# Rounding the weights' first part by a GpSimd casting transfer instead of ScalarE's copy

## The chip, the cores and the metric

The kernel runs on one core of one Trainium2 chip. The metric is the device time of one execution in microseconds (us), as the median of several runs. A profile is one separate execution with the hardware profiler on.

## The reference

Two layers of a hybrid model act on 256 context tokens and 256 latent tokens, each 2048 wide. A layer normalises and modulates its input to `u`, multiplies it by one wide weight matrix, sends groups of the product's columns through three mixers (a gated linear recurrence, a windowed attention, a state-space scan), and multiplies their joined outputs by a second matrix:

```python
u_l = rmsnorm(x, norm_w) * (1.0 + scale_l[:, None]) + shift_l[:, None]
u_c = rmsnorm(ctx_h, norm_w) * (1.0 + scale_c) + shift_c
lx_c, lg_c, q_c, k_c, v_c, ag_c, xbc_c, z_c, dt_c = split_cols(u_c @ w_in)
lx_l, lg_l, q_l, k_l, v_l, ag_l, xbc_l, z_l, dt_l = split_cols(u_l @ w_in)
lru_c, lru_l = rglru_mixer(...)
att_c, att_l = window_attention(...)
ssd_c, ssd_l = ssd_mixer(...)
mix_l = concatenate([lru_l * silu(lg_l), att_l * silu(ag_l), ssd_l])
x_new = x + gate_l[:, None] * (mix_l @ w_out)
if update_ctx:                       # every layer but the last
    mix_c = concatenate([lru_c * silu(lg_c), att_c * silu(ag_c), ssd_c])
    ctx_h = ctx_h + gate_c * (mix_c @ w_out)
```

The modulation (`scale`, `shift`, `gate`) is itself a product of a condition vector with a third, 2048 by 6144 matrix per layer.

## The kernel before

**Three products for one.** All data are 32-bit floats. For the two large products every operand is split into a first part, rounded to the format `float32r`, and a second part, the rest (also `float32r`). `mm3` then makes three matmuls per 128x128 weight block: first part by `u`'s first part, first part by `u`'s second part, second part by `u`'s first part.

**The weight stream.** `blocks` brings the weights in program order, in halves of a 128x1024 tile: 128 partitions by 512 columns, that is four weight blocks, 256 KB. There are 640 halves: 224 for `w_in` and 96 for `w_out` in each of two layers. For each half SyncE (SP) issues a load into a buffer `raw` (5 of them), ScalarE (ACT) copies `raw` to `hi` with rounding (line 242; 4 buffers), and VectorE (DVE) writes `lo = raw - hi` (line 243; 4 buffers). TensorE (PE) runs 12 matmuls on a half. `hi` and `lo` are free again when the last of them is done, `raw` when the subtraction is done. In the first layer a matmul has 512 columns; in the second most have 256, since the context half is not needed for `C`, `lg`, `z`, `q`, `ag` and for all of `w_out`. Here such halves are called narrow, the others wide.

**Stages.** In each layer the columns `B`, `C`, `x` come first, then `lx` and `lg` in turns (the recurrence, while the state-space core runs beside it), `z`, `k`, `v`, then `q` and `ag` in turns (attention), then `w_out` in three parts. In the first layer the modulation's weights are read while the first columns run (`ada_rows`, tiles `ar`), and `ada_wide` reads 256 more blocks of 256 KB (tiles `araw`) through VectorE later on.

**What sets the order.** PE's order is the program's: a planner with its own clock and a table of due times (`WAIT`) decides after each weight block which mixer step comes next. The other engines' orders are made by the scheduler when the program is built, from its own timeline; each engine then runs its list strictly in order. GpSimd (POOL) has 174 elementwise steps before the change, among them the recurrence's product (line 732), two steps on its result (744, 754), sums of squares (432), the attention's scaling of `prob` (873). All transfers are issued by SP.

The change touches `SHARED` (buffer counts), `blocks` and one call in `layer`. Lines behind `blocks` stand three higher in the changed kernel: 243 becomes 246, 732 becomes 735.

Of the kernel before, what the change touches and what calls it, by code (L numbers as in the profile page):

```python
# [9 lines left out]
F32R = mybir.dt.float32r  # L10
AF = mybir.ActivationFunctionType
# [3 lines left out]
P = 128  # L15
# [75 lines left out]
NW = KT * 7 * 8 // 8  # L91
# [20 lines left out]

SHARED = {}
for _tag, _bufs, _roles in [
        ("raw", 5, ("raw",)),
        ("ta", 4, ("lt0", "lt1", "prob", "xsw", "ar1")),
        ("tb", 2, ("cv", "qw", "v", "sq")),
        ("tc", 3, ("lh0", "lh1", "xs", "stage", "ar2")),
        ("td", 4, ("ao", "xc", "la2", "lgt", "agt", "cth", "diag", "dts", "xw", "dtraw", "rt1", "awsb", "cond32")),
        ("te", 1, ("rb", "ptch", "ssq")),  # L120
        ("t4", 3, ("BT", "CT", "Btok", "vh", "vl", "ptlh", "ar0")),
        ("bc", 4, ("bc", "dtw", "kh0", "kh1", "adac")),
        ("aw", 3, ("araw", "ww", "part0")),
        ("ee", 2, ("ee", "kl0", "kl1", "ar4")),
        ("H", 3, ("H", "ptll", "ptcl", "ar3")),
        ("bd", 2, ("gw", "qh", "ql", "part1")),
        ("sm", 6, ("spe", "sps", "spq", "dtr", "dtz", "dta", "acsT", "asb", "condt", "cond", "ea", "nlam", "cbm"))]:
    for _r in _roles:
        SHARED[_r] = (_tag, _bufs)


HB = 4
MIXERS_FIRST = {"lru_x": 150, "ssd_core": 150}
WAIT = {"B": (36.48, 14.89), "C": (28.19, 0.27), "x": (33.09, 10.71), "dt": (16.92, 0.59), "softplus":
        (19.41, 30.37), "acs": (0.94, 0.68), "core": (4, 5.2), "ada": (2.38, 5.97), "ada1": (1.17, 2.75), "z":
# [5 lines left out]
class Kernel:  # L141
# [88 lines left out]
        return self.cst[:, o:o + w]  # L230


    def blocks(self, src, n_tiles):
        nc = self.nc
        for i in range(n_tiles):
            whole = src[i].rearrange("p (b c) -> p b c", b=8)
            for h in range(2):
                part = self.t([P, 4, P], "raw")
                nc.sync.dma_start(out=part, in_=whole[:, 4 * h:4 * h + 4])
                hi = self.t([P, 4, P], "hi", HB, F32R)  # L240
                lo = self.t([P, 4, P], "lo", HB, F32R)
                nc.scalar.activation(out=hi, in_=part, func=AF.Copy)  # L242
                nc.vector.tensor_tensor(out=lo, in0=part, in1=hi.bitcast(F32), op=ALU.subtract)  # L243
                for b in range(4):
                    yield hi[:, b], lo[:, b]
# [709 lines left out]
    def layer(self, l, xs):  # L955
# [4 lines left out]
        self.core_done = False  # L960
        self.lru_h, self.att_o, self.parts_done, self.mixes = {}, {}, set(), {}
        t0 = lambda kind: 0 if l == 0 or kind in CTX_COLS else C
        wst = self.blocks(self.a["w_in"][l], NW)
        us = []

        rows = None
# [315 lines left out]
```

## Time and profile before

| what | value |
|---|---|
| median of 3 runs | 1828.84 us (1825.97 to 1830.53) |
| the profiled execution | 1825.69 us |
| its span in the trace | 1823.7 us |
| PE busy | 1762.9 us, 97% |
| DVE busy | 1406.0 us, 77% |
| ACT busy | 972.9 us, 53% |
| POOL busy | 215.5 us, 12% |
| transfers | 322.99 MB, mean 177 GB/s |

How to read it: busy times are of one profiled execution, and instructions that only issue transfers are not counted as busy. A busy PE is not a PE at its peak. A wait of an engine costs time only if PE, which carries the weight stream from the first half to the last, gets later by it.

### The profile page before, as it was taken

How to read it: one execution, taken by the hardware profiler on the slowest of the kernel's cores; microseconds unless marked ns; L12 is line 12 of the kernel's file. 1: busy time of each engine (PE TensorE's matmuls, PEld its weight loads, DVE VectorE, ACT ScalarE, POOL GpSimd, SP SyncE). 2: the span in 40 equal slices, each digit the busy share in tenths (PEclk: the TensorE clock that was granted, in tenths of full speed). 3: DMA queues.
4: the chain of work that ended last, by engine and by line, in shares of the span. 5: the costliest groups of instructions: out<-in, count | busy, mean ns of one | idle time of the engine just before them, and what ended most of it. 6: DMA issues, size and time to landing. Idle time of an engine off the chain costs nothing.

```text
span 1823.7 us, 30174 instructions
## 1 busy us (share of the span) xinstructions
PE 1762.9 (97%) x10522; PEld 1449.8 (79%) x10522; DVE 1406.0 (77%) x3117; ACT 972.9 (53%) x1798; POOL 215.5 (12%) x179
## 2 busy tenths in 40 slices
PE   7999999999999999999999999999989999999999
PEld 4677876667778778887888887888767788999999
DVE  4447769898898888889999536877788785788665
ACT  4324578688523354555232335544788863678443
POOL 0000111111110021212000020001122120121000
PEclk9999999999999999999999999999999999999999
DMA  9982333334675645557777433464343564554655
GB/s 359 389 299 66 123 104 104 122 122 144 230 222 179 189 153 184 173 174 239 229 225 225 144 122 107 140 197 148 99 134 113 173 220 137 182 180 153 218 185 179
DMA packets 186343, 322.99 MB, mean 177 GB/s; under 512 B 19120, under 2 KB 44624, under 8 KB 185552
## 3 DMA queue, kind: packets, MB, share of 16 engines
q1 hardware_dynamic: 186192, 321.09, 54.0%
q8 instruction: 82, 1.34, 0.3%
q14 instruction: 69, 0.57, 0.1%
HBM read 310.38 MB, written 10.63 MB: 176 GB/s over the span
## 4 chain that ended last, share of the span: by engine, by line
PE 71%; DVE 9%; issue 8%; ACT 6%; DMA 5%; POOL 1%; SPq 0%; ACTq 0%; DVEq 0%; POOLq 0%
PE acc L175 56%; PE mx L175 12%; PE ada L175 2%; DVE lo L243 2%; DMA bc<-acsD 2%; PE mx L171 1%; DVE araw L385 1%; ACT hi L242 1%; DVE ada L385 1%; DVE lh L735 1%; DMA araw<-in_adaw_dram 1%; DMA ar<-in_ada_dram 1%; DVE ee L1170 1%; ACT ww L1172 1%; ACT lt L717 1%
## 5 line engine op out<-in xcount | busy, mean ns | idle before, releaser
L175 PE MATMUL acc<-u,hi 128*128 128x512 f32 (+1 forms) x4800 | 1278.0, 355 | 3.8 <-ACT u L457 3.0
L175 PEld LDWEIGHTS acc<-u,hi 128*128 128x128 f32 x4800 | 837.5, 190 | 149.4 <-issue 33.2
L175 PE MATMUL acc<-u,lo 128*128 128x512 f32 (+1 forms) x2400 | 843.0, 351 | 7.9 <-DVE lo L243 7.8
L242 ACT ACTIVATE hi<-raw 128x512 fp32r<-128x512 f32 x640 | 397.5, 628 | 536.4 <-PE acc L175 401.3
L243 DVE TENSOR_TENSOR lo<-raw,hi 128x512 fp32r<-128x512 f32 x640 | 456.8, 717 | 185.9 <-ACT hi L242 175.3
L175 PEld LDWEIGHTS acc<-u,lo 128*128 128x128 f32 x2400 | 455.4, 190 | 73.1 <-DVE lo L243 12.9
L385 DVE SCALAR_TENSOR_TENSOR araw<-araw,adac 128x512 f32<-128x512 f32 x256 | 184.3, 720 | 6.2 <-DMA araw<-in_adaw_dram 3.9
L385 DVE SCALAR_TENSOR_TENSOR ada<-araw,adac 128x512 f32<-128x512 f32 x192 | 140.1, 730 | 13.2 <-DMA araw<-in_adaw_dram 6.7
L175 PE MATMUL mx<-u,hi 128*128 128x512 f32 (+1 forms) x320 | 98.8, 392 | 0.0
L1082 DVE SCALAR_TENSOR_TENSOR X<-acc,mod,X 128x256 f32<-128x256 f32 x144 | 65.0, 478 | 40.2 <-PE acc L175 40.2
L732 POOL TENSOR_TENSOR lt<-lt,ltl 128x512 f32<-128x512 f32 x32 | 45.9, 1457 | 327.2 <-ACT ltl L729 304.9
L873 POOL TENSOR_SCALAR prob<-prob,qrs 128x512 f32<-128x512 f32 (+1 forms) x48 | 58.2, 1228 | 214.0 <-ACT hi L242 123.9
L432 POOL TENSOR_TENSOR ssq<-ssq,sq 128x512 f32<-128x512 f32 (+1 forms) x26 | 34.0, 1310 | 308.1 <-ACT sq L428 308.1
L175 PEld LDWEIGHTS mx<-u,hi 128*128 128x128 f32 x320 | 55.9, 188 | 14.0 <-issue 4.6
L175 PE MATMUL mx<-u,lo 128*128 128x512 f32 (+1 forms) x160 | 60.7, 379 | 0.0
L516 POOL TENSOR_SCALAR X<-xs,prm 128x512 f32<-128x512 f32 (+1 forms) x16 | 16.3, 1024 | 362.0 <-DVE xs L494 357.5
L175 PE MATMUL mx<-xc,gw 64*64 64x512 f32 x128 | 41.7, 622 | 8.8 <-ACT lt L717 5.3
L428 ACT ACTIVATE sq<-X 128x256 f32<-128x256 f32 (+1 forms) x44 | 18.8, 452 | 54.5 <-DVE X L659 52.8
L1170 DVE SCALAR_TENSOR_TENSOR ee<-bc,nacs,ee 128x128 f32<-128x128 f32 x96 | 34.8, 418 | 14.8 <-DMA bc<-acsD 9.1
L776 POOL TENSOR_TENSOR qw<-qw,cst 128x256 f32<-128x256 f32 x20 | 23.1, 1156 | 195.6 <-DVE rt L775 168.9
L717 ACT ACTIVATE lt<-mx,gbh 128x512 f32<-128x512 f32 x64 | 42.2, 674 | 4.1 <-PE mx L175 4.0
L1169 ACT ACTIVATE ee<-bc,nacs 128x128 f32<-128x128 f32 x96 | 30.6, 391 | 17.7 <-DMA bc<-acsD 17.7
(240 smaller groups left out, 1946.1 us busy)
## 6 DMA issues: line engine op xcount, KB each, us to landing
raw<-in_w_in_dram SPq DMA_DIRECT2D x448, 256.0 KB, 2.8
araw<-in_adaw_dram SPq DMA_DIRECT2D x256, 256.0 KB, 3.1
raw<-in_w_out_dram SPq DMA_DIRECT2D x192, 256.0 KB, 3.0
ar<-in_ada_dram SPq DMA_DIRECT2D x84, 256.0 KB, 5.4
bc<-acsD SPq DMA_DIRECT2D x48, 256.0 KB, 3.9
ar<-in_ada_dram SPq DMA_DIRECT2D x22, 512.0 KB, 7.0
adac<-condD SPq DMA_DIRECT2D x28, 256.0 KB, 4.4
gw<-in_gates_dram SPq DMA_DIRECT2D x16, 256.0 KB, 2.9
```

The lines of the kernel that those rows point to most:

```text
L175: self.nc.tensor.matmul(out=out, lhsT=lhsT, rhs=rhs, start=start, stop=stop, **kw)
L242: nc.scalar.activation(out=hi, in_=part, func=AF.Copy)
L243: nc.vector.tensor_tensor(out=lo, in0=part, in1=hi.bitcast(F32), op=ALU.subtract)
L385: i = nc.vector.scalar_tensor_tensor(out=o, in0=raw, scalar=1.0, in1=row[c].rearrange("p t x -> p (t x)"), op0=ALU.mult, op1=ALU.mult, acc ...
L432: nc.gpsimd.tensor_tensor(out=self.ssq[0], in0=self.ssq[0], in1=sq, op=ALU.add)
L717: nc.scalar.activation(out=t, in_=pg[g], func=AF.Tanh, scale=0.5, bias=self.gb[:, 16 * g + 8 * d + m:16 * g + 8 * d + m + 1])
L732: nc.gpsimd.tensor_tensor(out=ti, in0=ti, in1=tl[:, d], op=ALU.mult)
L776: nc.gpsimd.tensor_tensor(out=dst, in0=src, in1=self.con("cos"), op=ALU.mult)
L873: nc.gpsimd.tensor_scalar(out=pr[j], in0=pr[j], scalar1=rs[:, j:j + 1], scalar2=1.0, op0=ALU.mult, op1=ALU.mult)
L1082: nc.vector.scalar_tensor_tensor(out=x[:, s], in0=acc[:, s.start - w0:s.stop - w0], scalar=mod[:, 2 * KT + m, c:c + 1], in1=x[:, s], op0=A ...
L1169: nc.scalar.activation(out=e[:, j], in_=bcs[0][:, j], func=AF.Identity, bias=k.nacs[:, f:f + 1])
L1170: nc.vector.scalar_tensor_tensor(out=e[:, j], in0=bcs[1][:, j], scalar=k.nacs[:, r:r + 1], in1=e[:, j], op0=ALU.add, op1=ALU.min)
```

## The change

`blocks` gets a number `own`. In tiles below it ACT rounds as before. In all others GpSimd issues a second transfer of the same half from DRAM into `hi`, whose destination type is `float32r`; the transfer itself casts. The subtraction on VectorE stays and now waits for two transfers. `own` is 20 tiles (40 halves) for the first layer's `w_in` and 0 for the second layer's `w_in` and for both `w_out`, so 600 of 640 halves take the new way. `raw` goes from 5 buffers to 3, `hi` from 4 to 6, `lo` stays at 4.

```diff
-        ("raw", 5, ("raw",)),
+        ("raw", 3, ("raw",)),
-HB = 4
-    def blocks(self, src, n_tiles):
+    def blocks(self, src, n_tiles, own=0):
                 part = self.t([P, 4, P], "raw")
                 nc.sync.dma_start(out=part, in_=whole[:, 4 * h:4 * h + 4])
-                hi = self.t([P, 4, P], "hi", HB, F32R)
-                lo = self.t([P, 4, P], "lo", HB, F32R)
-                nc.scalar.activation(out=hi, in_=part, func=AF.Copy)
+                hi = self.t([P, 4, P], "hi", 6, F32R)
+                lo = self.t([P, 4, P], "lo", 4, F32R)
+                if i < own:
+                    nc.scalar.activation(out=hi, in_=part, func=AF.Copy)
+                else:
+                    nc.gpsimd.dma_start(out=hi, in_=whole[:, 4 * h:4 * h + 4])
                 nc.vector.tensor_tensor(out=lo, in0=part, in1=hi.bitcast(F32), op=ALU.subtract)
-        wst = self.blocks(self.a["w_in"][l], NW)
+        wst = self.blocks(self.a["w_in"][l], NW, 0 if l else 20)
```

PE's list keeps its order. ACT's list in the second layer's recurrence: `lt`, `ltl` and `la` are the recurrence's gates, `bc` and `ee` belong to the state-space core, `hi` is the weights' first part. Before:

```order
L722 ACTIVATE ltl_13251<-lt_2949_13258,s_2638_11797 128x512
L717 ACTIVATE lt_2957_13286<-mx_13280,gbh_11799 128x512
L717 ACTIVATE lt_2958_13288<-mx_13281,gbh_11799 128x512
L723 ACTIVATE lt_2949_13258<-lt_2949_13258,s_2638_11797 128x512
L722 ACTIVATE ltl_13251<-lt_2957_13286,s_2638_11797 128x512
L242 ACTIVATE hi_13428<-raw_13426 128x512
L725 ACTIVATE la_2951_13264<-lt_2949_13258 128x512
L242 ACTIVATE hi_13450<-raw_13448 128x512
L723 ACTIVATE lt_2957_13286<-lt_2957_13286,s_2638_11797 128x512
L242 ACTIVATE hi_13468<-raw_13466 128x512
L725 ACTIVATE la_2959_13292<-lt_2957_13286 128x512
```

The same engine and place in the changed kernel:

```order
L725 ACTIVATE ltl_13251<-lt_2949_13258,s_2638_11797 128x512
L1178 ACTIVATE ee_13315<-ee_13315 128x512
L1183 ACTIVATE bc_13313<-bc_13313 128x512
L720 ACTIVATE lt_2957_13286<-mx_13280,gbh_11799 128x512
L726 ACTIVATE lt_2949_13258<-lt_2949_13258,s_2638_11797 128x512
L720 ACTIVATE lt_2958_13288<-mx_13281,gbh_11799 128x512
L725 ACTIVATE ltl_13251<-lt_2957_13286,s_2638_11797 128x512
L728 ACTIVATE la_2951_13264<-lt_2949_13258 128x512
L726 ACTIVATE lt_2957_13286<-lt_2957_13286,s_2638_11797 128x512
L728 ACTIVATE la_2959_13292<-lt_2957_13286 128x512
```

The copies to `hi` are gone from between the gates' steps.

POOL's list at the end of the second layer's recurrence, in the stage of `z`: `lt`, `lh` are the recurrence's tiles, `ssq` a sum of squares. Before:

```order
L732 TENSOR_TENSOR lt_3175_14363<-lt_3175_14363,ltl_14354 128x512
L732 TENSOR_TENSOR lt_3180_14385<-lt_3180_14385,ltl_14354 128x512
L744 TENSOR_TENSOR lh_3182_14395<-lh_3182_14395,lh_3183_14398 128x256
L754 TENSOR_TENSOR lh_3182_14395<-lh_3182_14395,lgt_14254 128x256
L432 TENSOR_TENSOR ssq_14575<-ssq_14575,sq_14675 128x256
```

The same engine and place in the changed kernel:

```order
L245 DMA hi_14554<-in_w_in_dram 128x512
L245 DMA hi_14580<-in_w_in_dram 128x512
L735 TENSOR_TENSOR lt_3175_14363<-lt_3175_14363,ltl_14354 128x512
L735 TENSOR_TENSOR lt_3180_14385<-lt_3180_14385,ltl_14354 128x512
L245 DMA hi_14598<-in_w_in_dram 128x512
L245 DMA hi_14616<-in_w_in_dram 128x512
L245 DMA hi_14634<-in_w_in_dram 128x512
L245 DMA hi_14681<-in_w_in_dram 128x512
L747 TENSOR_TENSOR lh_3182_14395<-lh_3182_14395,lh_3183_14398 128x256
L245 DMA hi_14726<-in_w_in_dram 128x512
L245 DMA hi_14744<-in_w_in_dram 128x512
L757 TENSOR_TENSOR lh_3182_14395<-lh_3182_14395,lgt_14254 128x256
```

The weight transfers now stand between the elementwise steps, before and behind each of them; `hi_14598` is the 398th of the 600, half number 437 counted from 0. The second such place, the product of `lt_3236` and `lt_3248`, has the 411th behind it, half number 450.

## Rows read from the trace of the kernel before

**Rows 1.** The page's head and its first part: busy us, share, instructions of an engine.

```profile
span 1823.7 us, 30174 instructions
PE 1762.9 (97%) x10522; PEld 1449.8 (79%) x10522; DVE 1406.0 (77%) x3117; ACT 972.9 (53%) x1798; POOL 215.5 (12%) x179
```

**Rows 2.** Stretches: length, each engine's busy us (instructions), PE's granted clock, DMA share, GB/s.

```profile
45.00:91.00 46.00, 45.07 (x500) 32.14 (x499) 22.16 (x59) 14.37 (x30) 0.00 (x0) 1.00 1.04 389
182.00:500.00 318.00, 306.85 (x1562) 227.85 (x1561) 265.98 (x529) 227.40 (x428) 52.36 (x40) 0.98 0.42 135
500.00:900.00 400.00, 389.02 (x1897) 321.87 (x1896) 356.70 (x903) 176.63 (x331) 59.46 (x48) 1.00 0.60 192
1100.00:1300.00 200.00, 195.03 (x972) 161.68 (x971) 146.54 (x322) 101.92 (x190) 12.53 (x11) 0.98 0.45 144
1300.00:1500.00 200.00, 184.65 (x1228) 146.61 (x1227) 169.53 (x298) 158.79 (x283) 43.16 (x37) 0.99 0.46 151
1700.00:1823.00 123.00, 120.36 (x1004) 120.15 (x1002) 78.54 (x131) 52.85 (x88) 0.00 (x0) 1.00 0.59 185
```

**Rows 3.** The page's groups: busy us, mean ns of one, idle before and releaser.

```profile
L242 ACT ACTIVATE hi<-raw 128x512 fp32r<-128x512 f32 x640 | 397.5, 628 | 536.4 <-PE acc L175 401.3
L243 DVE TENSOR_TENSOR lo<-raw,hi 128x512 fp32r<-128x512 f32 x640 | 456.8, 717 | 185.9 <-ACT hi L242 175.3
L732 POOL TENSOR_TENSOR lt<-lt,ltl 128x512 f32<-128x512 f32 x32 | 45.9, 1457 | 327.2 <-ACT ltl L729 304.9
```

**Rows 4.** Line 242 alone, in two stretches: ACT's busy us, clock, DMA share, GB/s.

```profile
182.00:500.00 318.00, 51.48 (x84) 0.98 0.42 135
1300.00:1500.00 200.00, 44.70 (x76) 0.99 0.46 151
```

**Rows 5.** The chain of waits from 1300 to 1500 us, shares by line.

```profile
by line: PE acc L175 23.7%; issue 20.1%; DVE lo L243 6.6%; DVE lh L735 5.0%; ACT hi L242 4.8%; PE mx L175 3.6%; DMA bc<-acsD 3.4%; DMA X<-xD 3.1%; ACT L729 2.5%; ACT lt L717 2.1%; DVE xc L471 2.1%; ACT ltl L729 1.9%; DVE lh L738 1.8%; ACT l
```

**Rows 6.** Transfers: the queue (packets, MB, share) and the weights' issues (median us to landing).

```profile
q1 hardware_dynamic: 186192, 321.09, 54.0%
...
raw<-in_w_in_dram SPq DMA_DIRECT2D x448, 256.0 KB, 2.8
...
raw<-in_w_out_dram SPq DMA_DIRECT2D x192, 256.0 KB, 3.0
```

**Rows 7.** POOL in order of time, stage of `z` in layer two: start, length, [idle before].

```profile
1454.54 2.99 POOL L732 TENSOR_TENSOR lt<-lt,ltl 128x512 f32<-128x512 f32 x2 [14.21 <-ACT ltl L729]
...
1478.71 3.01 POOL L732 TENSOR_TENSOR lt<-lt,ltl 128x512 f32<-128x512 f32 x2 [3.87 <-ACT ltl L729]
```

**Rows 8.** Instructions that touch `hi`, counted from the start: PE first (8 a half).

```profile
0.00:1459.40 1459.40, 1063.36 (x3496) 636.83 (x3497) 311.03 (x437) 271.65 (x439) 0.99 0.54 176
0.00:1481.90 1481.90, 1082.47 (x3600) 653.02 (x3601) 321.02 (x450) 279.47 (x452) 0.99 0.54 176
```

**Rows 9.** Instructions that touch `acc` in both `w_out` stages: PE, then weight loads.

```profile
900.00:950.00 50.00, 50.00 (x222) 41.42 (x221) 7.15 (x17) 0.00 (x0) 1.00 0.75 237
...
1700.00:1720.00 20.00, 20.00 (x170) 20.00 (x168) 3.31 (x7) 0.00 (x0) 1.00 0.57 180
```

**Rows 10.** Tile `raw` from 1700 us on: lengths in ns min/median/max, landing in us.

```profile
L243 DVE TENSOR_TENSOR lo<-raw,hi x81: 678/693/693, 1700.0 to 1815.2; 128x512 fp32r<-128x512 f32 x81
...
L239 SPq DMA_DIRECT2D raw<-in_w_out_dram x76: 327/328/489, 1700.7 to 1808.7; - x76
...
DMA to landing us min/median/max: 2.5/3.0/4.4
```

**Rows 11.** What PE waited for: us in total, times, longest us.

```profile
PE mx L175 <- ACT lt L717: 11.9, 8, 4.2
...
PE mx L171 <- POOL prob L873: 3.4, 4, 2.2
```

**Rows 12.** Tile `ar` from 45 to 91 us, where transfers are densest: landing in us.

```profile
DMA to landing us min/median/max: 4.8/5.9/7.7
```

## The prediction

> **What bounds the kernel now.** I read the page's head first: PE is busy for 1762.9 of 1823.7 us [rows 1], so 60.8 us of idle PE is nearly all that a change away from PE can win. The table of stretches comes next and says where the idle time lies [rows 2]: 318 - 306.85 = 11.2 us from 182 to 500 (first layer's recurrence and state-space core), 11.0 us from 500 to 900 (attention), 5.0 us from 1100 to 1300, 15.4 us from 1300 to 1500 (second layer's recurrence, `z`), 2.6 us in the last stage, of which the reader may take most for the kernel's end. The same rows hold a second, smaller loss: the granted clock is 0.98 of the upper level, 2.4 GHz, from 182 to 500 and from 1100 to 1300, and 0.99 from 1300 to 1500, that is 0.02 x 318 + 0.02 x 200 + 0.01 x 200 = 12.4 us, in stretches in which PE also idles.
>
> In both recurrences ACT and DVE are nearly full: 227 and 266 of 318 us, 159 and 170 of 200 us [rows 2]. The chain of waits from 1300 to 1500 agrees [rows 5]: matmuls into `acc` hold only 23.7% of it, the rest is spread over many ACT and DVE steps, 4.8% being ACT's copy to `hi` and 6.6% DVE's `lo`. The longest waits of PE by releaser are for ACT's gate step, 11.9 us in 8 times [rows 11]. From 1700 us on nothing of this kind is left: PE runs 168 weight loads in 20 us [rows 9], 0.119 us a matmul, 12 x 0.119 = 1.43 us a narrow half, and takes `w_out`'s 96 halves at that pace. In the first layer's `w_out` 221 loads take 50 us, which is 2.71 us a wide half.
>
> **What goes.** 600 of 640 copies leave ACT, 628 ns each [rows 3], 377 us in all. They cover work elsewhere, so what counts is the two recurrences: 51.5 us of ACT's 227.4 and 44.7 of its 158.8 [rows 4, 2], about a quarter of the load of an engine on which PE waits. DVE's wait for the copy, 175.3 us over the run [rows 3], goes with it. What is late next is DVE: it stays at 84 and 85% busy there, and all its 717 ns subtractions stay. So of the idle time from 182 to 500 and from 1100 to 1500, 31.5 us, the gain lies between nothing (DVE sets all of it) and all; I take half, 16 us, since the chain mixes the two engines' steps [rows 5]. Of the clock's 12.4 us I also take half, 6 us, with bounds of 0 and 12.4. The 11.0 us of the attention stage I leave at no gain (bounds 0 and 11), because ACT is only 44% busy there [rows 2]. Gain 22 us, bounds 0 and 55.
>
> **What comes: issues on POOL.** No transfer of the trace is issued by POOL; all went through SP's queue [rows 6]. So the price of one issue is bounded by SP's, 0.33 us [rows 10], and by POOL's own elementwise step, 1.46 us [rows 3]; landing by 2.8 to 3.0 us, a plain half's median [rows 6, 10], and 5.9 us, `ar`'s median where the queues are full [rows 12]. I take values close to the lower ends, as the queues are at 0.42 to 0.60 in all the stretches concerned [rows 2]. In the attention stage 400 / 2.71 = 148 issues cost POOL at most 216 us beside its 59 us of 400, so it does not fill up.
>
> *Order on POOL.* Its list is in order, and a transfer now queues behind elementwise steps that wait for ACT. For most places PE is far from needing that half. In the stage of `z` it is not. The first pair of products ends at 1454.54 + 2.99 = 1457.5 [rows 7]; behind it stands the transfer of half 437, and PE has finished with 3496 = 8 x 437 first-part matmuls at 1459.4 [rows 8], so it wants that half 1.9 us later. The second pair ends at 1481.7, half 450 (3600 = 8 x 450) is wanted at 1481.9, after 0.2 us. An issue and a landing take 0.33 + 2.8 = 3.1 us at the lower and 1.46 + 5.9 = 7.4 us at the upper end, so PE gets 1.2 + 2.9 = 4 us later, or 5.5 + 7.2 = 13 us. POOL waited 14.21 and 3.87 us for ACT's `ltl` before these pairs [rows 7]; a lighter ACT brings them earlier, which can take the loss to nothing. I take 5 us.
>
> *The other way round*, an elementwise step waits behind an issue, which itself waits for PE to free a buffer. PE waited for `prob` only 4 times [rows 11]: 4 x 0.33 = 1 us, at most 4 x 1.46 = 6 us. I take 1 us.
>
> *Buffers.* With six of `hi` a transfer starts when PE is through with the half six before; five halves of work remain, 5 x 1.43 = 7.15 us in the narrow stage. Issue, landing and subtraction take 0.33 + 3.0 + 0.69 = 4.0 us at the lower end [rows 10]: nothing is lost. At the upper end they take 1.46 + 5.9 + 0.69 = 8.05 us, and a half costs (8.05 + 1.43) / 6 = 1.58 us, 0.15 x 96 = 14 us more. I take 0; in wide halves there are 13.6 us and no loss at either end. `raw` with three buffers and `lo` with four still run 7 halves ahead, 10 us when narrow, against a landing of 3: 0 us. But SP now stops sooner at a `raw` that has no buffer, with the state-space core's `bc` loads queued behind; the chain gives `bc` 3.4% of 200 us [rows 5], so 0 to 7 us, taken as 0 since a `raw` frees as soon as its subtraction is done.
>
> **What comes: bytes.** 600 halves are read twice, 157 MB on top of 323. The densest stretch shows what the queues carry: 389 GB/s at a share of 1.04 from 45 to 91 us [rows 2]. At that rate 262,144 bytes take 0.67 us and the two reads of a narrow half 1.35 us, under PE's 1.43 us: 94% full, 0 us lost. For the wide stages it is no question: 192 GB/s from 500 to 900, plus 262 KB per 2.71 us = 97 GB/s, is 289 GB/s. A rule speaks against this: the Trainium skill (DMA: Bandwidth & Descriptors, Specifications) puts a core's share of the memory at about 358 GB/s, and says under "Issuing engines are not separate DMA queues" that transfers from another engine share the same 16 DMA engines. By it a narrow half would take an estimated 1.46 us and the sum would rise by 0.03 x 96 = 3 us. The 389 GB/s of the trace differ from that limit, and the measurement decides. The same page (Anatomy of one DMA, SWDGE path) gives a GpSimd transfer about 2.0 us plus its bytes at 436 GB/s, an estimated 2.6 us for a half; by that the loop above would keep its lower end. No run here shows it.
>
> **The sum.** -22 + 5 + 1 = -16 us. Against the profiled execution, 1825.69 us, that is 1810; this execution lies 3 us under the median of the runs, 1828.84, from which the forecast is counted: **1813 us**.
>
> **Rivals.**
>
> *DVE is the bound.* For it: DVE is the fuller engine in both recurrences [rows 2] and `lo` has the larger share of the chain [rows 5]. Against it: PE's longest waits are for an ACT step [rows 11]. Then about 6 us are won, 6 lost at POOL: 1829 us.
>
> *The last stage runs at the weights' pace* (slower). Place: the 96 narrow halves of the second layer's `w_out`, where nothing else covers a late half. A half has 1.43 us, the plain read takes 0.67 of it, so it decides from a casting read of 0.76 us, only 13% dearer than a plain one, or from 1.43 us of POOL per issue, which is just below its elementwise 1.46. For it: no row shows a casting transfer, the margin is thin, and all other places have slack that this one lacks. Against it: PE's pace there is even and the queues are at 0.59 now [rows 2, 9]. With a cast at 1.5 times a plain read a half takes 0.67 + 1.01 = 1.68 us, 0.25 x 96 = 24 us more: 1837; at twice, 0.59 x 96 = 57 us more: 1870. I put this rival at 1840 us, since late halves in `z` would add a little.
>
> That the change does not do what it says can be left aside: ACT's list keeps 40 copies of 640.
>
> **How the numbers follow.** About 0.3%, 5.5 us, is what a measurement here can tell from no change. The forecast, 1793 to 1823 us, has a chance of 0.50; no difference 0.15; the slower rival 0.35. So faster 0.50, same 0.15, slower 0.35. The range begins at 1793, where the recurrences' idle time and the clock's loss go whole (44 us) and the upper costs of POOL are met in part (8 us), and reaches into the slower rival to 1862, a cast of 1.9 times a plain read; beyond it I leave some 0.1, below it 0.05. The forecast's own range is 1793 to 1823.
>
> **What would show it.** Right: ACT near 600 us busy; PE's idle time from 1300 to 1500 down by about half; in the last stage still 1.43 us a half with a DMA share near 0.95; a few us of PE waiting for `hi` near the pairs of products in `z`. Wrong: PE waits before matmuls with `hi` from 1700 on, POOL's issues longer than 1.4 us, casting packets longer than plain ones, or the same idle time in the recurrences with DVE's steps as releasers.

## The result: 1920.55 us, 5.0% slower

| | before | after |
|---|---|---|
| median | 1829.68 us (1825.97 to 1830.69, 4 runs) | 1920.55 us (1919.89 to 1922.13, 4 runs) |
| ratio of after to before | | 1.0501, 95% interval 1.0484 to 1.0517 |
| span of the profiled execution | 1823.7 us | 1918.3 us |
| mean granted clock of PE | 0.993 | 0.984 |

The forecast was 1813 us, in a range of 1793 to 1862: the sign was wrong, and the range missed the time by 59 us. The page of after, head and first part, against [rows 1]:

```profile
span 1918.3 us, 30196 instructions
PE 1793.2 (93%) x10522; PEld 1462.7 (76%) x10522; DVE 1401.2 (73%) x3117; ACT 633.4 (33%) x1198; POOL 525.0 (27%) x779
```

ACT lost 339.5 us, as meant. PE's idle time rose from 60.8 to 1918.3 - 1793.2 = 125.1 us, and its same 10522 matmuls took 30.3 us longer. Of these an estimated 0.009 x 1918 = 17 us go with the lower granted clock. So 64 + 30 = 94 us is the whole loss of the span.

The stretches of after answer to [rows 2] (same columns; the work in a stretch has shifted):

```profile
182.00:500.00 318.00, 307.46 (x1589) 230.00 (x1588) 271.42 (x544) 185.47 (x346) 101.03 (x128) 1.00 0.70 209
500.00:900.00 400.00, 374.48 (x1781) 307.33 (x1780) 333.02 (x833) 104.28 (x203) 114.64 (x159) 0.98 0.81 252
1100.00:1300.00 200.00, 196.21 (x953) 164.47 (x952) 142.68 (x320) 54.05 (x112) 56.76 (x86) 0.98 0.79 239
1300.00:1500.00 200.00, 187.80 (x1160) 143.07 (x1159) 157.28 (x278) 125.36 (x211) 68.91 (x96) 0.97 0.73 217
1700.00:1918.00 218.00, 185.54 (x1434) 175.72 (x1432) 119.20 (x238) 28.06 (x65) 63.17 (x115) 0.99 0.93 282
```

The first recurrence is better than before: 1589 matmuls in place of 1562, at a granted clock of 1.00 in place of 0.98. From 500 us on it turns, and from 1700 us on PE is idle for 32.5 us where it was for 2.6. PE's largest wait is now for DVE's `lo`: 58.1 us in 57 times, against 7.8 us in 10. What DVE waits for has changed with it. Two groups of the page, against [rows 3], and POOL's new one:

```profile
L246 DVE TENSOR_TENSOR lo<-raw,hi 128x512 fp32r<-128x512 f32 x640 | 456.0, 716 | 240.1 <-DMA raw<-in_w_out_dram 75.8
L245 POOL DMA_DIRECT2D hi<-in_w_in_dram x408 | 221.7, 544 | 811.0 <-PE acc L174 530.1
L245 POOL DMA_DIRECT2D hi<-in_w_out_dram x192 | 102.4, 534 | 324.6 <-PE acc L174 282.1
```

The wait of DVE for ACT's copy has shrunk from 175.3 to 21.1 us (in the 40 halves that ACT still rounds), and its largest is now for the transfer of `raw` (75.8 us in `w_out`, 34.2 in `w_in`), not of `hi` (1.9 and 11.9). An issue on POOL takes 0.53 to 0.54 us. Queues and landings of the page (median us), against [rows 6]:

```profile
q1 hardware_dynamic: 186192, 321.09, 51.0%
q0 software_dynamic: 86400, 157.32, 29.6%
...
raw<-in_w_in_dram SPq DMA_DIRECT2D x448, 256.0 KB, 3.9
hi<-in_w_in_dram POOLq DMA_DIRECT2D x408, 256.0 KB, 4.3
araw<-in_adaw_dram SPq DMA_DIRECT2D x256, 256.0 KB, 4.3
raw<-in_w_out_dram SPq DMA_DIRECT2D x192, 256.0 KB, 4.5
hi<-in_w_out_dram POOLq DMA_DIRECT2D x192, 256.0 KB, 4.9
```

The landings became longer, those of SP's own plain loads too: `raw` from 2.8 and 3.0 to 3.9 and 4.5 us, `araw` from 3.1 to 4.3. The loads of `ar`, issued before 134 us, where ACT still rounds, land after 5.4 us as before.

**The last stage.** Tile `raw` of after from 1760 to 1910 us, in the form of [rows 10]:

```profile
L246 DVE TENSOR_TENSOR lo<-raw,hi x80: 678/691/694, 1761.3 to 1909.5; 128x512 fp32r<-128x512 f32 x80
L239 SPq DMA_DIRECT2D raw<-in_w_out_dram x79: 327/328/1083, 1762.0 to 1908.4; - x79
its engine sat idle before it (us, times) until:
  DMA raw<-in_w_out_dram: 65.5, 57
...
DMA to landing us min/median/max: 2.8/4.7/7.2
```

79 halves take 1909.5 - 1761.3 = 148.2 us, 1.88 us each, where the kernel before takes 1.44. The chain of waits of after shows why, from 1809 us on (start, length, what holds the chain):

```profile
1809.64 4.67 DMA raw<-in_w_out_dram
...
1814.43 0.70 DVE lo L246
...
1815.15 4.55 DMA raw<-in_w_out_dram
...
1819.82 0.70 DVE lo L246
...
1820.54 4.61 DMA raw<-in_w_out_dram
```

It is a closed loop: a load of `raw`, its subtraction, and then the load into the buffer that the subtraction freed. One turn takes 1815.15 - 1809.64 = 5.51 us, and three buffers make three halves of it: 1.84 us a half. PE is not in these turns; just before them it holds the chain for 4.36 us.

### The profile page after: what moved, and what is told of

The parts are those of the page before. It is cut to its first block, busy times and chain, and to the rows that moved or that the text cites. A ratio compares the mean times of both kernels' runs of the same rounds, so it can differ in the third digit from the quotient of the medians.

```text
span 1918.3 us, 30196 instructions
## 1 busy us (share of the span) xinstructions
PE 1793.2 (93%) x10522; PEld 1462.7 (76%) x10522; DVE 1401.2 (73%) x3117; ACT 633.4 (33%) x1198; POOL 525.0 (27%) x779
## 4 chain that ended last, share of the span: by engine, by line
PE 45%; DMA 22%; DVE 18%; issue 8%; ACT 5%; POOL 2%; DVEq 0%; SPq 0%; POOLq 0%; ACTq 0%
PE acc L174 31%; PE mx L174 11%; DMA raw<-in_w_out_dram 8%; DMA araw<-in_adaw_dram 6%; DVE lo L246 5%; DVE araw L388 3%; DMA raw<-in_w_in_dram 3%; DVE ada L388 3%; DMA bc<-acsD 3%; PE ada L174 2%; DMA hi<-in_w_in_dram 2%; DMA adac<-condD 1%; PE mx L170 1%; DVE X L1085 1%; DVE ee L1173 1%
## 5 line engine op out<-in xcount | busy, mean ns | idle before, releaser
L174 PE MATMUL acc<-u,lo 128*128 128x512 f32 (+1 forms) x2400 | 852.6, 355 | 58.4 <-DVE lo L246 58.1
L246 DVE TENSOR_TENSOR lo<-raw,hi 128x512 fp32r<-128x512 f32 x640 | 456.0, 716 | 240.1 <-DMA raw<-in_w_out_dram 75.8
L245 POOL DMA_DIRECT2D hi<-in_w_in_dram x408 | 221.7, 544 | 811.0 <-PE acc L174 530.1
L245 POOL DMA_DIRECT2D hi<-in_w_out_dram x192 | 102.4, 534 | 324.6 <-PE acc L174 282.1
L174 PE MATMUL mx<-u,lo 128*128 128x512 f32 (+1 forms) x160 | 60.8, 380 | 0.1
L876 POOL TENSOR_SCALAR prob<-prob,qrs 128x512 f32<-128x512 f32 (+1 forms) x48 | 49.3, 1040 | 12.7 <-DVE qrs L870 8.4
L702 ACT ACTIVATE xsw<-xc 64x512 f32<-64x512 f32 x32 | 20.2, 631 | 65.8 <-DVE xc L474 63.0
```

The costliest lines, as they stand in the source:

```text
L174: self.nc.tensor.matmul(out=out, lhsT=lhsT, rhs=rhs, start=start, stop=stop, **kw)
L245: nc.gpsimd.dma_start(out=hi, in_=whole[:, 4 * h:4 * h + 4])
L702: nc.scalar.activation(out=xs[r:r + 64], in_=xc[o:o + 64], func=AF.Copy)
L876: nc.gpsimd.tensor_scalar(out=pr[j], in0=pr[j], scalar1=rs[:, j:j + 1], scalar2=1.0, op0=ALU.mult, op1=ALU.mult)
```

## Experiments

Times are medians with the kernel before beside it on the same chip. Where a run has an interval, it is that of the ratio to before. To place a loss, I took from the records of each trace the start of the first matmul on a weight half and subtracted that of the kernel before, both counted from the span's start (half 112 lies at 468 us, 176 at 672, 320, the second layer's first, at 1118, 464 at 1506, 544, `w_out`'s first there, at 1677). The last column is the mean from half 560 to 630. e1 to e9, e15 and e16 ran once. Kernels whose median is that of before stand up to 7 us from it in such a single execution (e17), so smaller differences carry little.

| buffers raw/hi/lo, who rounds | us | 112 | 176 | 320 | 464 | 544 | 639 | us a half, last stage |
|---|---|---|---|---|---|---|---|---|
| before: 5/4/4, ACT | 1829.68 | 0 | 0 | 0 | 0 | 0 | 0 | 1.44 |
| after: 3/6/4, transfers | 1920.55 | -8 | 16 | 29 | 39 | 56 | 94 | 1.86 |
| e1: 3/6/4, ACT | 1877.33 | 10 | 26 | 26 | 33 | 42 | 52 | 1.52 |
| e2: 4/5/4, transfers | 1936.35 | 2 | 25 | 48 | 65 | 86 | 110 | 1.68 |
| e3: 5/4/4, transfers | 1997.04 | 11 | 29 | 59 | 93 | 119 | 171 | 1.93 |
| e4: after, sums of squares on DVE | 1916.3 | -9 | 6 | 14 | 30 | 47 | 91 | 1.89 |
| e5: 4/6/3, transfers | 1882.8 | -10 | 1 | 17 | 25 | 38 | 57 | 1.59 |
| e6: after, ACT in the last stage | 1881.4 | -8 | 15 | 26 | 29 | 45 | 56 | 1.51 |
| e9: 4/6/3, ACT | 1870.29 | 13 | 26 | 27 | 35 | 43 | 45 | 1.44 |
| e12: 3/4/6, ACT | 1848.65 | 2 | 8 | 9 | 17 | 18 | 25 | 1.49 |
| e13: 4/4/5, ACT | 1829.37 | 1 | 4 | 5 | 5 | 5 | 5 | 1.44 |
| e17: 4/4/3, ACT | 1830.04 | -4 | 0 | -1 | -7 | -5 | -3 | 1.46 |
| e18: 3/4/4, ACT | 1852.96 | 1 | 9 | 9 | 17 | 20 | 28 | 1.51 |

### The parts of the change

The buffers of the change alone, ACT rounding as before (e1):

```diff
-        ("raw", 5, ("raw",)),
+        ("raw", 3, ("raw",)),
-                hi = self.t([P, 4, P], "hi", HB, F32R)
+                hi = self.t([P, 4, P], "hi", 6, F32R)
```

> The kernel before with the buffer counts of the change (raw 3, hi 6), ACT still copies, nothing is read twice. Buffer theory: a raw buffer is held from its issue to the end of the subtraction, so three of them let one half through per (0.33 issue + 3.0 landing + 0.63 copy + 0.69 subtraction) / 3 = 1.55 us; the last stage's 96 narrow halves, at 1.43 us before, get slower by about 12 us, some more in the second layer's z and q: 1840 to 1850 us. Bytes theory (the second read and its dearer packets fill the queues): as before, 1829 within 4 us. POOL-order theory (transfers caught behind elementwise steps on POOL): as before too.

Measured: 1877.33 us beside 1827.7, above every forecast. Half of the loss, 50 us, comes without a single second read. In the last stage the loop of `raw` explains it: (0.33 + 2.9 + 0.63 + 0.69) / 3 = 1.52 us from issue, landing, copy and subtraction, as measured. The other 42 us before that stage it does not explain.

The casts with other shares of the thirteen buffers (e2 with 4, 5 and 4 of `raw`, `hi`, `lo`; e3 with those of before):

```diff
-        ("raw", 3, ("raw",)),
+        ("raw", 5, ("raw",)),
-                hi = self.t([P, 4, P], "hi", 6, F32R)
+                hi = self.t([P, 4, P], "hi", 4, F32R)
```

(e2: 4 and 5 in place of 5 and 4.)

> The changed kernel with raw 4, hi 5. Buffer theory: raw lets a half through per (0.33 + 4.7 + 0.69) / 4 = 1.43 us, hi per (0.53 + 4.9 + 0.69 + 1.43) / 5 = 1.51 us, instead of 1.83 us measured in the last stage; 30 us come back there, some 10 elsewhere: 1880 us. Bytes theory: 1915 to 1925 us, since the same bytes move. POOL-order theory: 1915 to 1925 us.

> The changed kernel with the buffer counts of before (raw 5, hi 4). Buffer theory: raw is free (1.14 us a half), but four hi buffers let a half through per (0.53 + 4.9 + 0.69 + 1.43) / 4 = 1.89 us, so the last stage stays as slow as in the changed kernel, 1.85 to 1.9 us a half, with the subtraction waiting for hi instead of raw: 1915 to 1930 us, slower than with raw 4 and hi 5. Bytes theory: the same as the changed kernel, 1920 us, and the same as raw 4 and hi 5.

Measured: 1936.35 and 1997.04 us, both above every forecast. So the exchange of buffers that costs so much is needed by the cast, and without it (e3) the loss nearly doubles, 169 us against 91. ACT's copy takes `hi` only when `raw` is there; a casting transfer takes it from its issue on, some 5 us earlier. With four buffers the loop is (0.53 + 4.9 + 0.69 + 1.43) / 4 = 1.89 us a half; e3 takes 1.93. With five it gives 1.51, but e2 takes 1.68, and what holds it was not followed up. DVE in e3 waits for `hi` (us, times, longest):

```profile
DVE lo L246 <- DMA hi<-in_w_in_dram: 89.3, 74, 4.1
```

One `raw` more and one `lo` less, the casts as in after (e5):

```diff
-        ("raw", 3, ("raw",)),
+        ("raw", 4, ("raw",)),
-                lo = self.t([P, 4, P], "lo", 4, F32R)
+                lo = self.t([P, 4, P], "lo", 3, F32R)
```

> The changed kernel with raw 4, hi 6, lo 3: the same room in all, one buffer from lo to raw. Buffer theory: both streams have enough in narrow halves, raw (0.33 + 4.7 + 0.69) / 4 = 1.43 us and hi (0.53 + 4.9 + 0.69 + 1.43) / 6 = 1.26 us, so the last stage goes from 1.83 to about 1.5 us a half, the queues' own limit, 8 packets of 85 and 8 of 99 ns, being 1.47: 30 us come back there and some 10 before: 1875 to 1890 us; three lo buffers can take a few us back in the recurrences. Bytes theory: the last stage stays above 1.7 us a half and the time at 1910 to 1925 us.

Measured: 1882.8 us beside 1830.38. The fourth `raw` gives back 38 of the 91 us, 19 in the last stage and 18 ahead of it (56 to 38). The loss that stays is 52 us.

### The last stage: the buffers or the second read

ACT rounds the second layer's `w_out` again, all else as in after (e6):

```diff
-        wo = self.blocks(self.a["w_out"][l], 48)
+        wo = self.blocks(self.a["w_out"][l], 48, 48 if l else 0)
```

> The changed kernel, but the second layer's w_out (96 narrow halves) is rounded by ACT again; raw 3, hi 6. Buffer theory: that stage runs at the 1.53 us a half of the kernel before with these buffers, 0.3 us a half less, 29 us come back: 1890 to 1895 us, and 14 us of the stage stay lost to raw's three buffers. Bytes theory: the stage goes back to 1.43 us a half, 38 us: 1882 us.

Measured: 1881.4 us; the stage costs 56 - 45 = 11 us in place of 38, with 1.51 us a half as in e1. So in this stage about 10 us are the three buffers with short landings, and the rest needs the second read. The time is the one that the bytes theory gave, but its 1.43 us a half was not reached: 11 us came back ahead of the stage (56 to 45), and why was not followed up.

Is it the read or the cast? In two kernels ACT rounds everything, but in the second layer's `w_out` GpSimd reads each half a second time, plain (e15) or with a cast (e16), and the subtraction takes this second copy:

```diff
-        ("raw", 5, ("raw",)),
+        ("raw", 3, ("raw",)),
-HB = 4
+HB = 3
                 nc.scalar.activation(out=hi, in_=part, func=AF.Copy)
+                if again:
+                    part = self.t([P, 4, P], "dm", 4, F32)
+                    nc.gpsimd.dma_start(out=part, in_=whole[:, 4 * h:4 * h + 4])
-        wo = self.blocks(self.a["w_out"][l], 48)
+        wo = self.blocks(self.a["w_out"][l], 48, l == 1)
```

(e16: `dm` of type `F32R`.)

> Only the last stage counts here. ACT rounds every half (three raw, three hi, three lo buffers, so the time of the whole is not to be compared), but in the second layer's w_out each half is read a second time by GpSimd, without a cast, into four buffers dm, and the subtraction takes dm in place of raw. A raw is then free after ACT's copy: (0.33 + landing + 0.63) / 3; a dm after the subtraction: (0.53 + landing + 0.69) / 4. Both theories start from the loop of the buffers with the landing as it comes. If a second read as such lengthens the landings: 3.9 us or more for raw from 1700 us on, and 1.62 us a half or more. If it is the cast: about 3.0 us, and 1.43 to 1.45 us a half.

> As the run with the plain second read, but the buffers dm have the type float32r, so that the transfer casts; the subtraction then gives zero, the weights' second parts of the second layer's w_out are left out. If the second read as such is what costs: the landings and the pace of the plain one within 5%. If casting is dearer (its packets took 18% more time than plain ones in the changed kernel): the dm landings longer than the plain ones by some 10 to 20%, and the pace slower by up to 0.15 us a half, 14 us in the stage.

Measured, the tile `raw` of e15 from 1740 to 1860 us:

```profile
L239 SPq DMA_DIRECT2D raw<-in_w_out_dram x65: 327/328/384, 1739.7 to 1859.8; - x65
...
DMA to landing us min/median/max: 2.9/4.8/6.6
```

and of e16:

```profile
L239 SPq DMA_DIRECT2D raw<-in_w_out_dram x64: 327/328/618, 1740.9 to 1859.1; - x64
...
DMA to landing us min/median/max: 3.0/4.7/6.5
```

The second copy lands after 5.2 us in both, and a half takes 1.86 and 1.87 us. The queues of the two pages (packets, MB, share) differ, first e15, then e16:

```profile
q0 software_dynamic: 7680, 25.17, 4.1%
```

```profile
q0 software_dynamic: 13824, 25.17, 4.8%
```

The cast breaks a half into 144 packets in place of 80 and takes 4.8 / 4.1 = 1.17 times the queue time. That delays nothing here: a plain second read lengthens the landings as much. The loop closes again, (0.33 + 4.8 + 0.63) / 3 = 1.92 us against 1.86. What lengthens the landings is that two 256 KB reads are on their way per half: in e15 with the queues at 0.88 to 0.91 from 1740 us on, so ahead of full. A second read issued by SP was not run, so what the issuing engine adds is open.

### Ahead of the last stage: room, or the lists

My first reading of e1 was room: `raw` and `lo` together let seven halves run ahead of PE in place of nine. A test with four `raw`, six `hi`, three `lo` and ACT's copies (e9):

```diff
-        ("raw", 5, ("raw",)),
+        ("raw", 4, ("raw",)),
-                hi = self.t([P, 4, P], "hi", HB, F32R)
-                lo = self.t([P, 4, P], "lo", HB, F32R)
+                hi = self.t([P, 4, P], "hi", 6, F32R)
+                lo = self.t([P, 4, P], "lo", 3, F32R)
```

> The kernel before with raw 4, hi 6, lo 3; ACT copies all, nothing is read twice. Buffer theory: four raw buffers let a half through per (0.33 + 3.0 + 0.63 + 0.69) / 4 = 1.16 us, under the 1.43 of narrow halves: the last stage loses nothing and the time is 1829 to 1836 us (three lo buffers cost a little in the recurrences). With the same buffers and the casting transfer the time was 1883 us; what stands between the two is then the second read, by its bytes and its longer landing, and POOL's list. If this run comes out at 1860 us or more, buffers explain that run too.

Measured: 1870.29 us beside 1830.82. The last stage is at its old pace, yet 40 us are lost ahead of it. That agreed with room, and two runs with nine halves ahead seemed to confirm it (three `raw`, four `hi`, six `lo`: e12; four, four, five: e13):

```diff
-        ("raw", 5, ("raw",)),
+        ("raw", 3, ("raw",)),
-                lo = self.t([P, 4, P], "lo", HB, F32R)
+                lo = self.t([P, 4, P], "lo", 6, F32R)
```

(e13: 4 and 5 in place of 3 and 6.)

> The kernel before with ACT's copies and the same thirteen buffers, dealt out otherwise: three of raw, four of hi, six of lo, so that nine halves may still run ahead of PE. Room theory: what costs time in the recurrences is the number of halves ahead of PE (raw plus lo), so these stay as before and only the last stage is longer, since three raw buffers turn over in (0.33 + 2.9 + 0.63 + 0.69) / 3 = 1.52 us in place of 1.43: 96 x 0.09 = 9 us, so 1836 to 1842 us. Raw theory: three buffers for transfers cost the time wherever the rest goes, so as with three raw, six hi, four lo: 1870 to 1880 us.

> The kernel before with ACT's copies, four buffers of raw, four of hi, five of lo: also nine halves ahead, one raw fewer. Room theory: as before, 1826 to 1833 us, the last stage at 1.43 to 1.44 us a half. Raw theory: as with four raw, six hi, three lo, 1865 to 1872 us.

Measured: 1848.65 us, ratio 1.0089 (1.0069 to 1.0109), between the two forecasts, and 1829.37 us, 0.9989 (0.9973 to 1.0004). But these two differ from e1 and e9 in a second thing: they have four `hi`, not six. So the room again, with four `hi` (e17: four `raw`, three `lo`; e18: three `raw`, four `lo`):

```diff
-        ("raw", 5, ("raw",)),
+        ("raw", 4, ("raw",)),
-                lo = self.t([P, 4, P], "lo", HB, F32R)
+                lo = self.t([P, 4, P], "lo", 3, F32R)
```

(e18: 3 in place of 4 for `raw`, `lo` as before.)

> The kernel before with ACT's copies, four buffers of raw, four of hi as before, three of lo: seven halves ahead of PE, but without the six hi buffers of the earlier run with raw four and lo three. Room theory: seven halves ahead cost as in that run, 1862 to 1872 us. List theory: six hi buffers let the scheduler place ACT's copies earlier in ACT's list, where they wait for a transfer with the gates' steps behind them, and that is what cost the time; with four hi buffers the list is nearly that of before, and the kernel takes 1828 to 1838 us.

> As the other run, with three buffers of raw and four of lo. Room theory: as with raw three, hi six, lo four, 1870 to 1880 us. List theory: as with raw three, hi four, lo six, 1845 to 1855 us, the three raw buffers being all that is left of the cost.

Measured: 1830.04 us, ratio 1.0009 (0.9997 to 1.002), and 1852.96 us, 1.0131 (1.0102 to 1.016). The room theory falls: seven halves ahead cost nothing with four `raw`. Two things cost, apart from each other. Three `raw` cost 18 to 24 us (e12, e18). Six `hi` cost 1870.29 - 1830.04 = 40 us with four `raw` and 1877.33 - 1852.96 = 24 us with three, although more buffers take nothing away.

How more buffers can cost is seen in ACT's waits (us, times, longest), of e9:

```profile
ACT hi L242 <- DMA raw<-in_w_in_dram: 319.8, 218, 6.7
ACT hi L242 <- DMA raw<-in_w_out_dram: 186.2, 132, 6.2
ACT hi L242 <- PE acc L175: 65.4, 39, 4.6
```

and of e17:

```profile
ACT hi L242 <- PE acc L175: 396.5, 275, 5.3
ACT hi L242 <- DMA raw<-in_w_in_dram: 70.3, 41, 5.1
```

In e17, as before the change, a copy mostly waits until PE frees a `hi`, and its `raw` has long landed. In e9 it has a buffer at once, and it waits for its load instead, 506 us in 350 times. The scheduler places a copy where its timeline has the buffer free, and with six that is earlier in ACT's list. The same place in the first recurrence, ACT in order of time, in e9 (start, length, idle before and releaser):

```profile
453.43 0.69 ACT L717 ACTIVATE lt<-mx,gbh 128x512 f32<-128x512 f32 x1
456.19 0.63 ACT L242 ACTIVATE hi<-raw 128x512 fp32r<-128x512 f32 x1 [2.07 <-DMA raw<-in_w_in_dram]
456.72 0.80 ACT L722 ACTIVATE ltl<-lt,s 128x512 f32<-128x512 f32 x1
...
468.13 0.78 ACT L465 ACTIVATE xc<-acc,prm 128x512 f32<-128x512 f32 x1 [1.86 <-PE acc L175]
475.64 0.63 ACT L242 ACTIVATE hi<-raw 128x512 fp32r<-128x512 f32 x1 [6.73 <-DMA raw<-in_w_in_dram]
478.35 1.28 ACT L699 ACTIVATE xsw<-xc 64x512 f32<-64x512 f32 x2 [2.08 <-DVE xc L471]
```

and in e17:

```profile
439.15 0.57 ACT L750 ACTIVATE lgt<-acc 128x512 f32<-128x512 f32 x1
439.63 0.67 ACT L717 ACTIVATE lt<-mx,gbh 128x512 f32<-128x512 f32 x1
440.39 0.81 ACT L722 ACTIVATE ltl<-lt,s 128x512 f32<-128x512 f32 x1
441.11 0.67 ACT L717 ACTIVATE lt<-mx,gbh 128x512 f32<-128x512 f32 x1
```

In e9 a copy stands between the gates' `lt` and `ltl` and holds the rest of the list for 2.07 us until its `raw` lands, and another one waits 6.73 us; in e17 the gates' steps run through at this place. That six `hi` cost 24 to 40 us is shown; that ACT's list is the way is read from these rows. Lists of the other engines change as well, and that was not taken apart.

### What relief for ACT is worth

The cast only where ACT is fullest, in the first layer's recurrence (36 tiles), ACT's copy elsewhere, with 4, 5 and 4 buffers (e7):

```diff
-    def blocks(self, src, n_tiles, own=0):
+    def blocks(self, src, n_tiles, cast=()):
-                if i < own:
+                if i not in cast:
                     nc.scalar.activation(out=hi, in_=part, func=AF.Copy)
-        wst = self.blocks(self.a["w_in"][l], NW, 0 if l else 20)
+        wst = self.blocks(self.a["w_in"][l], NW, () if l else range(20, 56))
```

> Only 72 halves are cast by transfers, those of the first layer's recurrence (tiles 20 to 55 of its w_in); all others by ACT; raw 4, hi 5, lo 4. Relief theory (a lighter ACT is worth something there): the stretch that gained 9 us in the changed kernel gains again and nothing is lost later: 1818 to 1824 us. Buffer theory: the stretch gained only with six hi buffers and gave 0 to 2 us with these counts; 1828 to 1836 us.

Measured: 1828.06 us beside 1830.38, no difference that one run could tell; no gain at half 112 (+3). The same with 4, 6 and 3 buffers (e10), and with 28 tiles of the second layer's head and recurrence as well (e11):

```diff
-                hi = self.t([P, 4, P], "hi", 5, F32R)
-                lo = self.t([P, 4, P], "lo", 4, F32R)
+                hi = self.t([P, 4, P], "hi", 6, F32R)
+                lo = self.t([P, 4, P], "lo", 3, F32R)
-        wst = self.blocks(self.a["w_in"][l], NW, () if l else range(20, 56))
+        wst = self.blocks(self.a["w_in"][l], NW, range(20, 48) if l else range(20, 56))
```

(The last line is e11's alone.)

> Only the first layer's recurrence (72 halves) is cast by transfers, all others by ACT; raw 4, hi 6, lo 3. Relief with enough buffers: the stretch gains 9 to 10 us as it did in the run with casting everywhere and these counts, nothing is lost later: 1818 to 1824 us, ratio 0.994 to 0.997. If the gain is given back by waits later in the recurrence or in z: 1829 us.

> As the run before it, and 56 halves of the second layer's head and recurrence are cast too. Relief: 3 us more than that run, 1815 to 1822 us; if narrow lg halves and POOL's list spoil it there, 1825 to 1835 us.

Measured: 1850.09 us, ratio 1.0106 (1.0084 to 1.0127), and 1853.11 us, 1.0116 (1.009 to 1.0142), both above every forecast. At half 112 e10 is 10 us ahead of before, as after (8), e4 (9) and e5 (10) are: all the kernels with six `hi` in which only transfers round there, apart from e11, which stands at 2. At half 176 e10 has lost it again (+3), and behind that ACT's copies run with six `hi`. The second recurrence gave nothing that shows (e11).

The copy by GpSimd's own elementwise step, buffers of before, in both recurrences (e8):

```diff
-                nc.scalar.activation(out=hi, in_=part, func=AF.Copy)
+                if i in pool:
+                    nc.gpsimd.tensor_copy(out=hi, in_=part)
+                else:
+                    nc.scalar.activation(out=hi, in_=part, func=AF.Copy)
```

> The kernel before with its buffers, and POOL instead of ACT copies raw to hi by an elementwise step in both recurrences (36 tiles of the first layer's w_in, 40 of the second's): ACT is relieved as in the changed kernel, with no second read and no change of buffers. Relief theory: the first recurrence gains 8 to 9 us, the second 5 to 10: 1810 to 1820 us. If DVE sets the pace there: 1829 us. If POOL's step, some 1.2 us against ACT's 0.63, and its in-order list come late: 1835 us and more.

Measured: 1831.13 us, where before took 1827.7 to 1830.8 in the runs told so far: no gain. Two stretches of 182 to 500 us, of e7:

```profile
182.00:500.00 318.00, 304.02 (x1556) 225.84 (x1556) 263.90 (x527) 191.95 (x357) 92.34 (x110) 0.98 0.64 191
```

and of e8:

```profile
182.00:500.00 318.00, 304.64 (x1556) 226.30 (x1555) 282.16 (x526) 191.47 (x357) 118.71 (x111) 0.98 0.42 133
```

ACT is relieved by the same 36 us in both. But in e8 DVE takes 18 us more for the same number of instructions while POOL copies, so that e8 does not tell what relief for ACT is worth; e7 has no such cost and gains nothing either. Last, every second half of the first recurrence by a cast, with all the buffers of before (e14):

```diff
-                if i not in cast:
+                if i not in cast or h:
```

> The buffers of before (five raw, four hi, four lo). Only in the first layer's recurrence, w_in tiles 20 to 55, the first half of each tile is rounded by GpSimd's transfer, the second by ACT: 36 halves. Room theory: nine halves ahead remain and a casting transfer holds one of four hi buffers for about 4 us longer, so part of ACT's relief is kept: 1823 to 1829 us. If a casting transfer needs more hi buffers even for every second half, the weight stream falls behind by 10 us or more in that stage: 1838 us and over.

Measured: 1833.27 us, ratio 1.0011 (1.0 to 1.0022): no gain. None of these kernels is shown to beat the kernel before.

### POOL's order

The running sum of squares goes from POOL to DVE, all else as in after (e4):

```diff
-            nc.gpsimd.tensor_tensor(out=self.ssq[0], in0=self.ssq[0], in1=sq, op=ALU.add)
+            nc.vector.tensor_tensor(out=self.ssq[0], in0=self.ssq[0], in1=sq, op=ALU.add)
```

> The changed kernel with the sums of squares on DVE instead of POOL (26 elementwise steps move). POOL-order theory: in the first layer's z POOL stood up to 11 us behind ACT's squares with the weights' transfers queued behind it, and the weight stream fell back by 20 us between halves 128 and 160; without these steps most of it comes back: 1895 to 1905 us. Buffer and bytes theories: the fall there is raw's three buffers or the queues, and 1915 to 1925 us.

Measured: 1916.3 us, 4 less than after; the order on POOL was to give 1895 to 1905. What it removes is seen in POOL's time line of after, in the first layer's `z`:

```profile
565.15 1.54 POOL L435 TENSOR_TENSOR ssq<-ssq,sq 128x512 f32<-128x512 f32 x1 [9.34 <-ACT sq L431]
566.64 2.17 POOL L245 DMA_DIRECT2D hi<-in_w_in_dram  x4
575.16 0.54 POOL L245 DMA_DIRECT2D hi<-in_w_in_dram  x1 [6.36 <-PE acc L174]
```

The sum waits 9.34 us for ACT, and then four weight transfers go out in one go that had been held behind it. Without it 10 us are won by half 176 and 15 by half 320, but only 9 are left at half 544 and 3 at the end. Why the last stage took 6 us more there than in after was not followed up.

## Why the prediction was wrong

**The step that failed: "Buffers".** It says that "`raw` with three buffers and `lo` with four still run 7 halves ahead, 10 us when narrow, against a landing of 3: 0 us". Seven halves ahead are indeed enough where ACT rounds (e17). But three of them can be in flight or on the way to their subtraction at a time, since a subtracted half has left `raw`. The same step worked the loop of `hi` at both its ends and forgot to do it for `raw`: at the lower end (0.33 + 3.0 + 0.69) / 3 = 1.34 us, under PE's 1.43, and at the upper one, with the 5.9 us of [rows 12], (0.33 + 5.9 + 0.69) / 3 = 2.31 us, 0.88 x 96 = 84 us in the last stage. Such a bound of 0 to 84 us would have held what the stage lost; the prediction put the term at 0. Measured: landing 4.7, 1.88 us a half, 38 us.

**Landing: mis-sized.** Taken were 2.8 to 3.0 us, because the queues stood at 0.42 to 0.60; the casts themselves bring them to 0.70 to 0.93. It was 3.9 to 4.9 us, between the ends, and it was longer for `araw` too (3.1 to 4.3). The Trainium skill (DMA: Bandwidth & Descriptors, Anatomy of one DMA, SWDGE path) gave an estimated 2.6 us for a half; the 4.3 and 4.9 us of this trace do not agree, and the measurement decides: the landing here is 1.7 to 1.9 times that.

**Bytes: the rate was not reached, and its cost is not only the rate.** The sum took 389 GB/s, 1.35 us for two reads, under 1.43. In e5, with a fourth `raw`, the queues stand at a share of 1.05 and move less (1760 to 1820 us, as [rows 2]):

```profile
1760.00:1820.00 60.00, 55.67 (x437) 54.17 (x436) 34.82 (x62) 2.83 (x8) 19.12 (x37) 0.97 1.05 329
```

At 329 GB/s two reads take an estimated 1.59 us, and e5 takes 1.59 us a half; the loop of its four `raw` gives less, (0.33 + 4.9 + 0.69) / 4 = 1.48. So the bytes may well hold it there, but that was not taken apart. And "94% full, 0 us lost" left out that transfers near full queues land later, which a loop with few buffers pays in full (e15).

**What more buffers do to a list: not thought of.** "With six of `hi`" was looked at as room alone. Six of them cost 24 to 40 us where ACT rounds (e1, e9 against e18, e17). In after ACT rounds only 40 halves, so this sum cannot simply be carried over to it.

**The gain: right in its place, wrong in its worth.** The first recurrence became 8 to 10 us faster, but mostly by the clock's term. From the start of half 40 to that of half 112 PE runs the same matmuls, before and after (as [rows 2]):

```profile
187.80:468.20 280.40, 269.25 (x1392) 198.61 (x1391) 232.76 (x463) 204.01 (x394) 44.26 (x34) 0.98 0.40 128
188.80:460.10 271.30, 263.04 (x1392) 195.42 (x1391) 230.88 (x466) 168.85 (x323) 83.73 (x106) 1.00 0.68 202
```

Of the 9.1 us, 6.2 are shorter busy time at a granted clock of 1.00 in place of 0.98 (e17, without casts, has 0.99 there and is 4 us ahead at half 112), and only 2.9 are idle time (11.2 to 8.3), the term that the sum had put at 16 us in both recurrences. Over the whole execution the clock's term even has the other sign, 0.993 to 0.984. The second recurrence gave nothing that shows (after, e11). And the gain was seen with six `hi` alone: with five the same 36 us less of ACT give nothing at half 112 (e7), nor does the cast everywhere (e2). Whether DVE holds the rest, as the rival "DVE is the bound" had it, no run settled.

**POOL.** Issues: 0.53 us, within 0.33 to 1.46. The second layer's `z`: from half 420 to 464 after loses 9 us and e1, without casts, 4. That the 5 us between them are the term as taken is luck: it is no more than such a difference can tell, and the place is not the one that was named. PE's waits at halves 437 and 450 of after (start, length, idle before):

```profile
1489.02 0.38 PE L174 MATMUL acc<-u,lo 128*128 128x256 f32 x1 [0.28 <-DVE lo L246]
...
1517.91 0.39 PE L174 MATMUL acc<-u,lo 128*128 128x256 f32 x1 [1.15 <-DVE lo L246]
```

The kernel before waits 0.60 and 1.60 us there. What holds the chain from 1500 to 1545 us are loads of `raw` (32.3%) and a transfer of `hi` behind a sum of squares (4.78 us from 1508.05 on). The first layer's `z` was passed over, with "For most places PE is far from needing that half": 10 to 15 us (e4), held by a sum of squares.

**The slower rival**, given 0.35, had place and sign, but not the cause. By its sum the last stage slows from a cast of 1.13 times a read on. The cast costs 1.17 times the queue time (e16), for which that sum gives 0.02 x 96 = 2 us; and it adds no landing time of its own. The loop of three buffers at 4.7 us made the 38.

**Where the 91 us went** (94 in the profiled execution), as far as it is settled: 38 in the last stage, 7 to 11 of them for three `raw` at the old landing (e12, e18, e1, e6) and the other 27 to 31 for the second read, by the longer landing (e15). Ahead of it 56 net of a gain of 8: a fourth `raw` gives back 18 (e5), sums of squares on DVE 9 to 15 (e4, most of it given back in the last stage). Open is the share of the rest: the longer landings of `araw` and of the state-space core's `bc`, and what six `hi` do to POOL's and DVE's lists where transfers round.

## What to carry to other kernels

For every buffer in a stream write down its own loop, (issue + landing + each step until it is free) / buffers, at both ends of the landing, and reckon with the upper end if the change itself loads the queues; the number of pieces that run ahead does not replace it. A casting transfer saves an engine's copy but holds its destination from its issue on and doubles the reads, so it wants more buffers of both kinds. And where a scheduler sets the lists, a buffer count is not only room: it moves work in the lists, so test it alone.

## What the runs showed of the hardware

- A second, plain read of each half lengthened the landing of the first from 3.0 to 4.8 us with the queues at 0.88 to 0.91 and 284 to 299 GB/s. That is well below the 389 GB/s of [rows 2]. With the cast and four `raw` (e5) the queues moved 329 GB/s at 1.05; where the limit of this mix lies was not measured.
- A 256 KB transfer issued by GpSimd took 80 packets when plain and 144 when it cast to `float32r`, with 17% more queue time, and landed after 5.2 us either way.
- While POOL copied weights in its own elementwise steps, DVE's instructions took 18 us more in 264 (e8 against e7); its subtractions took 815 ns in place of 738 (means from 182 to 500 us).
- An issue on POOL shows 0.53 us, the landing 4.3 to 4.9. The Trainium skill (Perfetto Trace Analysis, DMA Instruction — SWDGE (GPSIMD)) says that the profiled end is that of writing the descriptors, not of the data; the trace agrees.
